# Two heads' products by turns: RWKV backs, block inversion and S5 output in a hybrid S5/RWKV-7 block

## The chip, the cores and the metric

The kernel runs on one core of a Trainium2 chip. The metric is the device time of one execution in microseconds (us). A core has a tensor engine for matrix products (PE; its weight loads are listed as PEld), a vector engine (DVE), a scalar engine (ACT), a general engine (POOL, GpSimd) and a queue engine (SP), each working through its own instructions in the order in which the program was written. PE writes its results to PSUM, which has eight banks; DVE and ACT read them from there.

## The reference, cut to what matters

One layer of a flow-matching block over 256 latent tokens and 256 context tokens, width 2048. A combined projection feeds an S5 branch (64 groups of 16 channels, 64 complex states each, both directions) and an RWKV-7 branch (16 heads of 64, both directions); gates, an output projection and a gated feed-forward part follow.

```
bu = jnp.einsum('lbgh,gph->lbgp', ugc, bbar)
states = s5_scan(bu, abar, s0[di])
y = y + jnp.real(jnp.einsum('lbgp,ghp->lbgh', states, cm))
...
def step(s, inp):
    r_t, w_t, k_t, v_t, kk_t, a_t = inp
    s_kk = jnp.einsum('bhvk,bhk->bhv', s, kk_t)
    s = s * w_t[:, :, None, :] - s_kk[..., None] * (kk_t * a_t)[:, :, None, :] + v_t[..., None] * k_t[:, :, None, :]
    return s, jnp.einsum('bhvk,bhk->bhv', s, r_t)
```

The kernel works out both recurrences over chunks: four tokens a chunk in S5, 64 tokens a chunk in RWKV, where the step inside a chunk becomes products with a 64 x 64 matrix and the inverse of a triangular one.

## The kernel before

**Dense stream.** All large projections run as one stream of weight tiles through PE. Each tile of 128 x 128 is split by ACT (`hi`) and DVE (`lo`) and used in three passes into accumulators `psacc`. In the order of time the stream holds the input projection (weights `win`), the modulation vector (weights `adaR`, used unsplit: a product of one column of `sc` with 256 columns of weights `w`, 768 instructions in the trace), the gated projection of S5 (`glu`), and the later projections. The input projection has 4 banks for `psacc` and 4 for everything else; the modulation part has 2 and 6.

**Background streams.** The S5 branch and the RWKV branch are Python generators that name the engine on which they go on, and how many free banks they need (`"tensor:1"`). `drive` writes them and the dense stream into one program; a rough clock of the engines in the code (class `Clock`) decides only what is written next. Once written, the order on each engine is fixed.

**S5 output** (`s5_out`). Eight slabs, one bank `psyp` each. A slab has four pairs of groups; the even group of a pair lies in partitions 0 to 63, the odd one in 64 to 127 (the parity, `par`). Each parity takes five products of 64 x 64 into its own half of the bank's partitions: one of `W` with `u`, and four of `wout` with the states `SB`.

**RWKV.** The work goes by pairs of heads, p = 0 to 7 for the context and 8 to 15 for the latent tokens, in both directions d; two pairs make a half (`h0` to `h7`). One head of a pair lies in partitions 0 to 63, the other in 64 to 127.

- `rw_front` makes the scaled vectors `H` and `KR` of a pair and direction, on ACT and DVE.
- `rw_back` makes the products inside the chunks: for each head four transposes (`ident`, in tile `cst`) and four products `H` x `KR`, of 64 rows by 128 columns. In the context one bank a head holds both (`pshg`); in the latent part, transposes (`pshp`) and products (`psgp`) have a bank each. ACT and DVE then take the results out. I call one call of it a back: 32 in all, 16 per segment.
- `rw_invert` inverts the triangular matrices of two halves, four times in all: a substitution of 31 steps on DVE (tiles `lth`, `Nh`), then products of 32 x 32 on PE, into `pswp` and, after a copy by ACT, into `pswq`; two banks (x = 0, 1) of each, with 16 products for either head in a bank.
- `rw_chain` carries the state over the four chunks of a half, with products `psxp`, `psup`, `pssp` and, in the latent part, `psy1` and `psy2`. Two halves run side by side.
- Halves 4 and 5 need the room of halves 0 and 1 (`rw_room`), so latent fronts begin after the first chains; pairs 4 to 7 of the context need room that comes free at the end of the input projection.

An fp32 product shows in the trace as two PE instructions with a weight load each; I call them passes. A transpose is one pass.

Of the kernel before, what the change touches and what calls it, by code (L numbers as in the profile page):

```python
# [17 lines left out]
P = 128  # L18
D = 2048
KT = 16  # L20
T = 256
C = 64
# [77 lines left out]
def lay_out(i):  # L100
    """Arrange the inputs for the program's loads: reshapes, transposes and copies only."""
# [78 lines left out]
class Clock:  # L180
    """A rough clock of the engines while the program is written: only the order of emission
    rests on it, never the result."""

    def __init__(self):
        self.t = dict(tensor=0.0, vector=0.0, scalar=0.0, gpsimd=0.0, sync=0.0)
        self.dma = self.hw = 0.0
        self.w = {}
        self.r = {}
        self.mark = 0.0
        self.table = None  # L190
        self.mms = 0
        self.tick, self.cols, self.full = 0, 0.0, False
        self.recent = deque()

    def array(self, t0, cost, cols):
        """Time of a product by the tensor engine's clock, which rests after a window of little use."""
        i = int(t0 / 3.4133)
        if i != self.tick:
            self.full = i == self.tick + 1 and self.cols >= 3060
            self.tick, self.cols = i, 0.0  # L200
        self.cols += cols
        cost = cost if self.full else 2 * cost
        self.recent.append((t0 + cost, cols))
        return cost

    def use(self, t):
        """Columns that have gone through the tensor engine in the window before t."""
# [13 lines left out]
    def cost(self, eng, op, out, a, k):  # L221
# [3 lines left out]
        if eng == "tensor":  # L225
# [7 lines left out]
            # the weights' way in counts as well  # L233
# [17 lines left out]
    def run(self, eng, op, a, k):  # L251
# [29 lines left out]
        if eng == "tensor":  # L281
            n = 1
# [67 lines left out]
class Dense:  # L350
    """Streams weights through the tensor engine: each weight tile is split exactly into two
    float32r parts and used in three passes; the activations come split the same way."""
# [24 lines left out]
    def open(self, first, cap, side=None):  # L377
        """Rings for the weights of the half-units from `first` up to `cap`, loaded and split ahead of
        their use."""
# [19 lines left out]
    def open_raw(self, pool, first, cap):  # L399
        """Loads in `pool` for the half-units that are used as they are."""  # L400
# [13 lines left out]
    def prep(self):  # L414
        """Split the next weight tile; a stream."""
# [19 lines left out]
    def evacuate(self):  # L435
        """Take the sums out, one after another; a stream."""
# [8 lines left out]
    def drop(self):  # L445
        """The sum has been read."""
        self.opened -= self.now
# [13 lines left out]
    def when(self):  # L461
        """When the weights of the next step will be there."""
# [5 lines left out]
    def step(self):  # L468
        """Emit a part of a half-unit: SUB weight tiles."""
# [39 lines left out]
class Bg:  # L509
    """A background stream: yields the engine that its next operations start on (with a + when others  # L510
    may go first), or a condition."""
# [22 lines left out]
class Flags(dict):  # L534
    """What has been emitted so far, with the time at which it will have come about."""
# [17 lines left out]
class Kernel:  # L553
# [24 lines left out]
    # y = 1/sqrt(v): exp(-ln/2), then one Newton step.  # L578
# [8 lines left out]
    def run(self):  # L587
        nc, tc, A = self.nc, self.tc, self.A
        es = ExitStack()
        with es:  # L590
# [31 lines left out]
            # scratch in DRAM  # L622
# [17 lines left out]
    # ------------------------------------------------------------------ dense jobs  # L640
    def make_jobs(self):
# [27 lines left out]
        # the first two features by turns: the last parts of the activations come late  # L669
# [22 lines left out]
    # ------------------------------------------------------------------ helpers  # L692
# [17 lines left out]
    def drive(self, until, must=(), all=True, span=None, stop=lambda: False, drain=True):  # L710
        """Interleave the dense stream, up to half-unit `until`, with the background streams; spread
        over `span`, if given, so that it lasts as long as they do."""
        d, c = self.dense, self.clk
        p0, t0 = d.pos, c.t["tensor"]
        while ((all and (d.pos < until or (drain and d.busy()))) or any(not b.done for b in must)) and not stop():
# [11 lines left out]
            # small products alone don't keep the tensor engine's clock up  # L727
# [3 lines left out]
            if dense and pick is not None and not pick.cond:  # L731
                # products that would wait for their weights hold up what comes after them
# [16 lines left out]
    def after(self, t):  # L749
        """Let the stream go on once what was written to `t` has landed."""  # L750
        self.clk.mark = max(self.clk.mark, self.clk.w.get(t.tensor.name, 0.0))

    def add_banks(self, es, n):
        """Banks that the background streams share."""
# [6 lines left out]
    def bank(self, shape, name):  # L761
        """The bank that has been free for longest."""
# [16 lines left out]
    def e_mod(self, b, acc):  # L779
        """Two features of the modulation that the later parts take, from a row to columns."""  # L780
# [16 lines left out]
    def mod_late(self, pool):  # L797
        """The rest of the modulation vector: a product along the weights' rows for every feature."""
# [33 lines left out]
    # ------------------------------------------------------------------ startup  # L832
    def startup(self, sp):
# [5 lines left out]
        # the parts of the modulation's weights, every fourth for the vector engine, and what comes  # L839
        # between them  # L840
# [46 lines left out]
        # 1 / rms of every token, the same on all partitions  # L887
# [46 lines left out]
        def scales(k0, n):  # L934
            # ada (raw products) + bias; A1 = norm1_w * (1 + scale)
# [77 lines left out]
    # ------------------------------------------------------------------ z evacuation  # L1013
# [11 lines left out]
    def mix(self, acc, mu, ctx=None):  # L1025
        """z + (neighbour mean - z) * mu for one 128-channel tile."""
# [70 lines left out]
    def z_gate(self, m, acc):  # L1097
        """The gates are kept as tanh(z / 2): sigmoid(z) = (tanh(z / 2) + 1) / 2."""
# [8 lines left out]
    # ------------------------------------------------------------------ S5  # L1107
    def small_exp(self, pool, x, out, tag):
        """exp on a small tile: range reduction and a polynomial, good to float32."""
# [33 lines left out]
    def s5_prep(self):  # L1143
# [17 lines left out]
        def out_matrices():  # L1161
            # output matrix: Re(C L^t s): rows re and -im
# [32 lines left out]
        # sine and cosine of a_im * dt through the half angle  # L1195
# [24 lines left out]
        # powers of abar (1..4), abar - 1 and the factor of the input matrix  # L1220
# [25 lines left out]
        # recurrence factors, laid as the states are: [re/im][gp][dir]  # L1246
# [5 lines left out]
        # power tables by slot: B: forward 3 - j, backward j; C: forward t + 1, backward 4 - t  # L1252
# [24 lines left out]
        def turned():  # L1277
            # transposed input matrix, the two groups of a pair in diagonal blocks, and the kernel's lags
# [40 lines left out]
            # y += d * u, as a part of the zero-lag block  # L1319
# [5 lines left out]
            # matrix inside a chunk: both directions' blocks, moved to the token that they belong to  # L1325
# [47 lines left out]
    def s5_in(self):  # L1373
        """What enters the states in every chunk, of both segments at once."""
# [54 lines left out]
    def s5_states(self):  # L1429
        """States after each chunk; the backward direction runs over the chunks from the end. Of the  # L1430
        context only the last state counts: chunks are joined in pairs, level by level."""
# [52 lines left out]
    def s5_out(self, pool, SB, u, W):  # L1484
# [13 lines left out]
        for sl in range(8):  # L1498
            yield "tensor:1", wos[2 * sl], wos[2 * sl + 1], u
            yp = self.bank([P, 4, 64], f"psyp{sl}")  # L1500
            for g in range(4):
                gp = 4 * sl + g
                wo = wos[gp // 2]
                for par in range(2):
                    ps = slice(64 * par, 64 * par + 64)
                    nc.tensor.matmul(yp[ps, g, :], lhsT=W[ps, gp, :], rhs=u[ps, gp, :], start=True, stop=False)
                    for d in range(2):
                        for ri in range(2):
# [12 lines left out]
    # ------------------------------------------------------------------ RWKV-7  # L1521
    # Halves of four heads go through the streams one after another: `front` and `back` prepare each
    # pair of heads, the chunk matrices of two halves are inverted together, the state is carried
    # over the chunks, and `post` finishes the output of the latent halves.
    def rw_norm(self, j):
        """Keys of a pair of heads in both segments, normalised per head."""
# [32 lines left out]
    def rw_load(self, st, a):  # L1559
        """Loads of one pair of heads."""  # L1560
# [25 lines left out]
    def rw_front(self, st, a, d):  # L1586
        """Everything of one pair of heads in one direction that doesn't need the state, up to the
        scaled vectors."""
# [67 lines left out]
    def rw_bonus(self, st, a):  # L1656
        """Sum over the head of r * (k_fwd + k_bwd) * r_k, times v."""
# [24 lines left out]
    def rw_tiles(self, st):  # L1682
        """What a half keeps for its state."""
# [16 lines left out]
    def rw_room(self):  # L1700
        """Room for the halves: all of the context's at first; latent ones as the context's end, the
        last in the place of the first."""
# [30 lines left out]
    def rw_vt(self, st, a):  # L1733
        """Values of one pair, transposed."""
# [25 lines left out]
    def rw_back(self, st, a, d):  # L1760
        """Products inside the chunks of one pair in one direction."""
# [10 lines left out]
        # every product into a bank comes before the first read of it, and each head has its banks:  # L1772
        # the two heads' rows go through the array side by side
        for h in range(2):
            oth = hs[1 - h]
            yield "tensor:1" if W == C else "tensor:2", H, KR[h]
            if W == C:
                bank = self.bank([P, 2, 4, C], f"pshg{n_}_{h}")
                hp, gps, held = bank[:, 0], bank[:, 1], [bank]
            else:  # L1780
                hp = self.bank([P, 4, C], f"pshp{n_}_{h}")
                gps = self.bank([P, 4, W], f"psgp{n_}_{h}")
                held = [hp, gps]
            for u in range(4):
                nc.tensor.transpose(hp[:, u, :], lhs(h, u), self.cs("ident")[hs[h], hs[h]])
            for u in range(4):
                nc.tensor.matmul(gps[:, u, :], lhsT=lhs(h, u), rhs=KR[h][hs[h], a, d, u, :], start=True, stop=True)
# [8 lines left out]
            # the substitution reads A^T below its diagonal only  # L1796
# [8 lines left out]
    def rw_invert(self, sts):  # L1805
        """T = (I + A)^-1 of every chunk of two halves: 32 x 32 blocks on the diagonal by substitution
        with a problem on each partition, the block below by two products; T^T replaces A^T."""
# [593 lines left out]
```

## Time and profile before

| | us |
|---|---|
| three runs | 2313.3, 2315.94, 2323.11 |
| median of the runs | 2315.94 |
| profiled execution, span of its trace | 2319.3 |
| PE busy | 2235.1 (96%) |
| DVE busy | 1484.2 (64%) |
| ACT busy | 1103.1 (48%) |

The profiled execution is described by its span, from its first instruction to its last; no other time belongs to it. It lies 3.4 us above the median of the runs and inside their extent. All rows further down are of this execution, and times in them count from its start. Three stretches matter: the S5 output at 645 to 712 us, the rest of the input projection to 803 us, and the RWKV recurrence beside the modulation product to 1277 us.

### The profile page before, as it was taken

To read this page: it belongs to the slowest core of one execution; us is meant where nothing else is said; L and a number is where in the kernel's file an instruction comes from. 1 tells how busy PE (TensorE), PEld (TensorE's weight loads), DVE (VectorE), ACT (ScalarE), POOL (GpSimd) and SP (SyncE) were. 2 spreads that over 40 slices of the span, in tenths; PEclk is the share of its full clock that TensorE was granted. 3 is DMA by queue.
4 is the path that set the end of the run, shared out by engine and by line. 5 is a ranking of instruction groups with operands and counts; after the bars stand their busy time and mean duration, and the time that the engine had idled before them with its cause. 6 is when DMAs were issued, how large, how long until landed. Compare 5 with 4: busy or idle time off the path is not lost.

```text
span 2319.3 us, 46718 instructions
## 1 busy us (share of the span) xinstructions
PE 2235.1 (96%) x19036; PEld 1966.2 (85%) x19036; DVE 1484.2 (64%) x2899; ACT 1103.1 (48%) x1908; POOL 150.9 (7%) x313
## 2 busy tenths in 40 slices
PE   7999999999999999999989799999999999999997
PEld 2289999999999865565736699999999999999997
DVE  3778848889835746677482557666666666554444
ACT  2335664334646657474635544454444444443333
POOL 0001210000101102010010100000000000000000
PEclk9999999999999979888898899999999999999999
DMA  9945565367764434535162675667777776556653
GB/s 372 341 145 189 197 203 181 110 193 213 231 196 131 131 115 120 163 97 173 56 196 87 184 256 183 183 207 227 228 229 227 229 226 182 182 182 183 183 183 133
DMA packets 155063, 431.92 MB, mean 186 GB/s; under 512 B 26272, under 2 KB 39584, under 8 KB 153952
## 3 DMA queue, kind: packets, MB, share of 16 engines
q1 hardware_dynamic: 130192, 360.76, 49.9%
q0 software_dynamic: 17600, 57.17, 7.6%
q10 hardware_dynamic: 7056, 11.01, 1.4%
q8 instruction: 149, 2.44, 0.4%
q14 instruction: 66, 0.54, 0.1%
HBM read 398.46 MB, written 30.41 MB: 185 GB/s over the span
## 4 chain that ended last, share of the span: by engine, by line
PE 77%; DVE 8%; issue 7%; ACT 4%; DMA 4%; POOL 0%; ACTq 0%; SPq 0%; DVEq 0%; POOLq 0%
PE psacc L312 63%; PE adacc L312 2%; PE psyp L312 2%; DVE lo L312 1%; PE pshg L312 1%; PE psbu L312 1%; DMA w<-in_win_dram 1%; PE pswph L312 1%; DMA ad<-in_adaP_dram 1%; PE psgp L312 1%; PE pswqh L312 1%; PE psss L312 1%; PE pslb L312 1%; DVE Nh L312 1%; PE psuph L312 1%
## 5 line engine op out<-in xcount | busy, mean ns | idle before, releaser
L312 DVE TENSOR_TENSOR lo<-w,hi 128x1024 fp32r<-128x1024 f32 x478 | 584.8, 1224 | 421.5 <-ACT hi L312 412.8
L312 ACT ACTIVATE hi<-w 128x1024 fp32r<-128x1024 f32 x478 | 504.8, 1058 | 679.5 <-PE psacc L312 566.2
L312 PE MATMUL psacc<-h,hi 128*128 128x258 f32 x2816 | 511.1, 284 | 1.2 <-ACT hi L312 1.2
L312 PEld LDWEIGHTS psacc<-h,hi 128*128 128x128 f32 x2816 | 438.4, 190 | 1.4 <-ACT hi L312 1.4
L312 PE MATMUL psacc<-hl,hi 128*128 128x256 f32 x2144 | 407.4, 284 | 0.0
L312 PE MATMUL psacc<-h,lo 128*128 128x258 f32 x1408 | 400.1, 284 | 0.8 <-DVE lo L312 0.8
L312 PEld LDWEIGHTS psacc<-hl,hi 128*128 128x128 f32 x2144 | 332.4, 191 | 6.3 <-issue 5.7
L312 PE MATMUL psacc<-hl,lo 128*128 128x256 f32 x1072 | 303.5, 283 | 0.4 <-DVE lo L312 0.4
L312 PEld LDWEIGHTS psacc<-h,lo 128*128 128x128 f32 x1408 | 267.6, 190 | 1.0 <-DVE lo L312 1.0
L312 PE MATMUL psacc<-hid,hi 128*128 128x256 f32 x1408 | 253.5, 283 | 0.0
L312 PEld LDWEIGHTS psacc<-hid,hi 128*128 128x128 f32 x1408 | 219.9, 192 | 0.0
L312 PE MATMUL psacc<-w,sc 128*1 128x256 f32 x768 | 201.3, 407 | 19.1 <-DVE ada L312 8.5
L312 PEld LDWEIGHTS psacc<-hl,lo 128*128 128x128 f32 x1072 | 204.7, 191 | 0.6 <-DVE lo L312 0.6
L312 PE MATMUL psacc<-hid,lo 128*128 128x256 f32 x704 | 199.5, 283 | 0.0
L312 PE MATMUL psacc<-hc,hi 128*128 128x256 f32 x832 | 173.0, 289 | 0.0
L312 PEld LDWEIGHTS psacc<-w,sc 128*1 128x1 f32 x768 | 57.8, 86 | 125.3 <-DMA w<-in_adaR_dram 22.7
L312 PEld LDWEIGHTS psacc<-hid,lo 128*128 128x128 f32 x704 | 135.4, 192 | 0.0
L312 PEld LDWEIGHTS psacc<-hc,hi 128*128 128x128 f32 x832 | 127.8, 189 | 2.3 <-issue 1.4
L312 PE MATMUL psacc<-hc,lo 128*128 128x256 f32 x416 | 116.2, 279 | 0.0
L312 PE MATMUL psacc<-gl,hi 128*128 128x256 f32 x512 | 99.0, 295 | 11.1 <-ACT hi L312 6.0
L312 PE MATMUL adacc<-ad,sc 128*2 128x512 f32 x192 | 88.3, 612 | 17.2 <-DMA ad<-in_adaP_dram 9.7
L312 PEld LDWEIGHTS psacc<-gl,hi 128*128 128x128 f32 x512 | 83.8, 200 | 13.2 <-ACT hi L312 6.2
(368 smaller groups left out, 3465.4 us busy)
## 6 DMA issues: line engine op xcount, KB each, us to landing
w<-in_w_dram SPq DMA_DIRECT2D x264, 512.0 KB, 4.3
w<-in_win_dram SPq DMA_DIRECT2D x134, 512.0 KB, 4.2
w<-in_adaR_dram SPq DMA_DIRECT2D x192, 256.0 KB, 2.9
ad<-in_adaP_dram SPq DMA_DIRECT2D x48, 512.0 KB, 6.8
w<-in_glu_dram SPq DMA_DIRECT2D x32, 512.0 KB, 4.0
w<-in_wo_dram SPq DMA_DIRECT2D x32, 512.0 KB, 3.6
adg<-in_adaG_dram POOLq DMA_DIRECT2D x32, 512.0 KB, 5.3
ad<-in_adaD_dram SPq DMA_DIRECT2D x16, 512.0 KB, 7.7
```

Of the source, the lines that this page charges most:

```text
L312: return f(*a, **k)
```

## The change

In the backs, the products of the two heads are written by turns, products ahead of transposes, and the stream asks for the banks of both heads at once: two in the context, four in the latent part. In the block inversion the loop over heads moves inside the loop over the 16 blocks, and in the S5 output the loop over parities inside that over the products. The code's rough clock counts the products of a back at 0.55 of their cost. The rest of the diff takes comments out.

```
+        self.side = 1.0
...
         c = self.cost(eng, op, out, a, k)
         if eng == "tensor":
+            c *= self.side
...
# s5_out
-                for par in range(2):
-                    ps = slice(64 * par, 64 * par + 64)
+                pss = [slice(64 * par, 64 * par + 64) for par in range(2)]
+                for ps in pss:
                     nc.tensor.matmul(yp[ps, g, :], lhsT=W[ps, gp, :], rhs=u[ps, gp, :], start=True, stop=False)
-                    for d in range(2):
-                        for ri in range(2):
+                for d in range(2):
+                    for ri in range(2):
+                        for ps in pss:
...
# rw_back
+        yield "tensor:2" if W == C else "tensor:4", H, KR[0], KR[1]
+        hps, gs, holds = [], [], []
         for h in range(2):
-            oth = hs[1 - h]
-            yield "tensor:1" if W == C else "tensor:2", H, KR[h]
             if W == C:
                 bank = self.bank([P, 2, 4, C], f"pshg{n_}_{h}")
...
-            for u in range(4):
-                nc.tensor.transpose(hp[:, u, :], lhs(h, u), self.cs("ident")[hs[h], hs[h]])
-            for u in range(4):
-                nc.tensor.matmul(gps[:, u, :], lhsT=lhs(h, u), rhs=KR[h][hs[h], a, d, u, :], start=True, stop=True)
...
+        self.clk.side = 0.55
+        for u in range(4):
+            for h in range(2):
+                nc.tensor.matmul(gs[h][:, u, :], lhsT=lhs(h, u), rhs=KR[h][hs[h], a, d, u, :], start=True, stop=True)
+        for u in range(4):
+            for h in range(2):
+                nc.tensor.transpose(hps[h][:, u, :], lhs(h, u), self.cs("ident")[hs[h], hs[h]])
+        self.clk.side = 1.0
+        for h in range(2):
+            hp, gps, held, oth = hps[h], gs[h], holds[h], hs[1 - h]
...
# rw_invert, pswp (and pswq in the same way)
-            for h in range(2):
-                r0 = slice(64 * h, 64 * h + 32)
-                r1 = slice(64 * h + 32, 64 * h + 64)
-                for u in range(16):
+            for u in range(16):
+                for h in range(2):
+                    r0 = slice(64 * h, 64 * h + 32)
+                    r1 = slice(64 * h + 32, 64 * h + 64)
                     nc.tensor.matmul(wp[r1, u, :], lhsT=AQ[x][r0, u, 32:64], rhs=t11[r0, :, 16 * x + u],
                                      start=True, stop=True, tile_position=(64 * h, 64 * h + 32))
```

The order of instructions is the same in both programs up to the first back, but for the turns in `psyp`. Here are PE's rows at that first back, in the input projection just after the S5 output; the numbers after `pshg` are pair, direction and head, and a last number counts tiles. Before:

```order
L312 MATMUL psss_8200<-nk_8032,cst 128x512
L312 MATMUL pshg_0_0_0_8210<-cst,H_0_0_8193 128x64 x4
L312 MATMUL pshg_0_0_0_8210<-KR0h_8184,H_0_0_8193 128x64 x4
L312 MATMUL pshg_0_1_0_8221<-cst,H_0_1_8196 128x64 x4
L312 MATMUL pshg_0_1_0_8221<-KR0h_8184,H_0_1_8196 128x64 x4
L312 MATMUL psvt_0_8231<-cst,v_0_6642 128x128 x2
...
L312 MATMUL pshg_0_0_1_8255<-cst,H_0_0_8193 128x64 x4
L312 MATMUL pshg_0_0_1_8255<-KR1h_8185,H_0_0_8193 128x64 x4
```

After, in the same place:

```order
L315 MATMUL psss_8200<-nk_8032,cst 128x512
L315 MATMUL pshg_0_0_0_8210<-KR0h_8184,H_0_0_8193 128x64
L315 MATMUL pshg_0_0_1_8211<-KR1h_8185,H_0_0_8193 128x64
...
L315 MATMUL pshg_0_0_0_8210<-cst,H_0_0_8193 128x64
L315 MATMUL pshg_0_0_1_8211<-cst,H_0_0_8193 128x64
...
L315 MATMUL psvt_0_8230<-cst,v_0_6642 128x128 x2
```

Before, the second head of pair 0 came twelve dense instructions and a transpose of values later; now it takes turns with the first, and the other direction's back has moved further down. From here on the order of the background streams differs throughout. The place that moves most is the end of the context's RWKV work: PE's rows around the last back of the context (`pshg0_7_1`) and the last step of the first two chains (`psxp…_3`, `pssp…_3`), with the numbers of half and step in the names. Before:

```order
L312 MATMUL psxph1_3_10315<-SV0h1_8337,KR0h1_8332 64x64
...
L312 MATMUL pshg0_7_0_1_10324<-KR1h3_9603,H00_7_0_10240 128x64 x4
L312 MATMUL psuph1_3_10335<-xsh1_3_10333,AQh1_8334 64x64 x8
...
L312 MATMUL pssph1_3_10370<-SV0h1_8337,HT0h1_8335 64x64
...
L312 MATMUL psmod2_10414<-cst_74,arow_79 128x1 x2
...
L312 MATMUL pshg0_7_1_0_10500<-KR0h3_9602,H10_7_1_10459 128x64 x4
L312 MATMUL pslb1_0_1_10514<-wad1_98,lw1_0_10162 128x256 x2
...
L312 MATMUL pshg0_7_1_1_10520<-KR1h3_9603,H10_7_1_10459 128x64 x4
```

After:

```order
L315 MATMUL psmod2_10255<-cst_74,arow_79 128x1 x2
...
L315 MATMUL pshg0_7_1_0_10358<-KR0h3_9460,H10_7_1_10314 128x64
L315 MATMUL pshg0_7_1_1_10359<-KR1h3_9461,H10_7_1_10314 128x64
...
L315 MATMUL pslb1_0_1_10383<-wad1_98,lw1_0_10144 128x256 x2
L315 MATMUL psxph0_3_10390<-SV0h0_8189,KR0h0_8184 64x64
...
L315 MATMUL psuph1_3_10439<-xsh1_3_10430,AQh1_8486 64x64 x8
...
L315 MATMUL pssph1_3_10471<-SV0h1_8489,HT0h1_8487 64x64
...
L315 MATMUL psmod3_10541<-cst_74,arow_79 128x1 x2
```

The context's last back stood behind the first chains' last step and now stands ahead of it, while the modulation product (`psmod` counts its features) has come equally far. In later inversions and chains the streams keep nearly the same places to each other.

## Rows read from the trace of the kernel before

**Rows 1.** Windows: length; busy us (PE, PEld, DVE, ACT, POOL); PEclk; DMA; GB/s

```profile
645.00:712.00 67.00, 66.77 (x815) 62.42 (x813) 19.79 (x28) 26.09 (x38) 5.35 (x10) 1.00 0.65 188
712.00:803.00 91.00, 89.22 (x707) 83.06 (x706) 66.90 (x131) 67.79 (x136) 14.14 (x33) 0.98 0.43 135
803.00:1277.00 474.00, 445.23 (x4642) 276.64 (x4642) 286.79 (x745) 257.71 (x591) 48.00 (x106) 0.88 0.41 125
```

**Rows 2.** Chain that ended last, two slabs of S5 output: start us, us, what

```profile
667.46 5.32 PE psyp L312 x66
672.78 2.34 PE psacc L312 x18
```

**Rows 3.** Timeline of PE, first slab of S5 output: start us, us, engine, instruction

```profile
648.55 0.33 PE L312 MATMUL psyp<-u,W 64*64 64x64 f32 x2
648.71 0.71 PE L312 MATMUL psyp<-SB,wout 64*64 64x64 f32 x5
649.15 0.27 PE L312 MATMUL psyp<-u,W 64*64 64x64 f32 x1
...
649.31 0.71 PE L312 MATMUL psyp<-SB,wout 64*64 64x64 f32 x7
649.75 0.27 PE L312 MATMUL psyp<-u,W 64*64 64x64 f32 x1
```

**Rows 4.** Timeline of PE, one head of a context back, and what follows

```profile
716.99 0.46 PE L312 MATMUL pshg<-cst,H 64*128 64x64 f32 x4 [0.31 <-ACT HT0h L312]
717.29 1.05 PE L312 MATMUL pshg<-KR1h,H 64*128 64x64 f32 x8
718.27 0.51 PE L312 MATMUL psacc<-hl,hi 128*128 128x256 f32 x2
```

**Rows 5.** Timeline of PE, two heads of a latent back that stand side by side

```profile
907.05 0.27 PE L312 MATMUL psgp<-KR0h,H 64*128 64x128 f32 x1
907.07 0.22 PE L312 MATMUL pshp<-cst,H 64*128 64x64 f32 x1
907.13 0.33 PE L312 MATMUL psgp<-KR1h,H 64*128 64x128 f32 x1
907.16 0.27 PE L312 MATMUL psgp<-KR0h,H 64*128 64x128 f32 x1
```

**Rows 6.** Timeline of PE, products of the first inversion

```profile
832.62 3.56 PE L312 MATMUL pswph<-t11h,AQh 32*32 32x32 f32 x64
...
844.05 2.11 PE L312 MATMUL pswqh<-AQh,w1h 32*32 32x32 f32 x64
...
849.17 3.43 PE L312 MATMUL pswqh<-AQh,w1h 32*32 32x32 f32 x64
```

**Rows 7.** Windows of tile pswp, then of pswq, in the recurrence

```profile
803.00:1277.00 474.00, 28.22 (x512) 27.23 (x512) 9.41 (x16) 0.88 0.41 125
...
803.00:1277.00 474.00, 25.74 (x512) 24.82 (x512) 9.39 (x16) 0.88 0.41 125
```

**Rows 8.** Timeline of PE, one step of a chain: both heads' products into one bank

```profile
870.98 0.68 PE L312 MATMUL psuph<-xsh,AQh 64*64 64x64 f32 x16
871.59 0.27 PE L312 MATMUL psxph<-SV0h,KR0h 128*64 128x64 f32 x1
871.60 0.27 PE L312 MATMUL psxph<-SV1h,KR1h 128*64 128x64 f32 x1
```

**Rows 9.** Windows of the recurrence: inversions' products, substitutions and chains by turns

```profile
857.70:900.00 42.30, 42.28 (x537) 30.89 (x536) 20.39 (x54) 31.40 (x85) 4.65 (x11) 0.88 0.24 69
900.00:963.90 63.90, 57.21 (x299) 26.25 (x300) 54.33 (x144) 30.12 (x69) 10.36 (x21) 0.95 0.63 192
963.90:990.00 26.10, 26.10 (x299) 19.88 (x298) 3.00 (x7) 12.24 (x22) 2.28 (x6) 0.56 0.22 67
...
1028.00:1087.30 59.30, 52.77 (x292) 25.95 (x290) 54.58 (x143) 28.55 (x64) 10.07 (x22) 1.00 0.64 189
...
1151.00:1224.50 73.50, 64.36 (x340) 29.13 (x338) 57.71 (x135) 33.90 (x61) 6.20 (x11) 1.00 0.58 182
```

More of the change, by code (lines that the diff above doesn't have):

```diff
@@ L1771, in rw_back @@
         lhs = lambda h, u: H[hs[h], u].rearrange("p s t -> p (s t)")[:, h * C:h * C + P]
+        yield "tensor:2" if W == C else "tensor:4", H, KR[0], KR[1]
+        hps, gs, holds = [], [], []
         for h in range(2):
-            oth = hs[1 - h]
-            yield "tensor:1" if W == C else "tensor:2", H, KR[h]
             if W == C:
                 bank = self.bank([P, 2, 4, C], f"pshg{n_}_{h}")
-                hp, gps, held = bank[:, 0], bank[:, 1], [bank]
-            else:
-                hp = self.bank([P, 4, C], f"pshp{n_}_{h}")
-                gps = self.bank([P, 4, W], f"psgp{n_}_{h}")
-                held = [hp, gps]
-            for u in range(4):
-                nc.tensor.transpose(hp[:, u, :], lhs(h, u), self.cs("ident")[hs[h], hs[h]])
-            for u in range(4):
-                nc.tensor.matmul(gps[:, u, :], lhsT=lhs(h, u), rhs=KR[h][hs[h], a, d, u, :], start=True, stop=True)
+                hps.append(bank[:, 0])
+                gs.append(bank[:, 1])
+                holds.append([bank])
+            else:
+                hps.append(self.bank([P, 4, C], f"pshp{n_}_{h}"))
+                gs.append(self.bank([P, 4, W], f"psgp{n_}_{h}"))
+                holds.append([hps[h], gs[h]])
+        self.clk.side = 0.55
[8 more added lines that the diff above has]
+            hp, gps, held, oth = hps[h], gs[h], holds[h], hs[1 - h]
             mask = self.cs("mask")
@@ L1871, in rw_invert @@
             wp = self.bank([P, 16, 32], f"pswq{n_}_{x}")
-            for h in range(2):
-                r0 = slice(64 * h, 64 * h + 32)
-                r1 = slice(64 * h + 32, 64 * h + 64)
-                for u in range(16):
+            for u in range(16):
+                for h in range(2):
+                    r0 = slice(64 * h, 64 * h + 32)
+                    r1 = slice(64 * h + 32, 64 * h + 64)
                     nc.tensor.matmul(wp[r0, u, :], lhsT=w1[r1, 16 * x + u, :], rhs=AQ[x][r1, u, 32:64], start=True, stop=True,
```

## Prediction

> **What bounds the kernel now.** I first read the windows of three stretches [rows 1]: how long each engine worked in the S5 output, the rest of the input projection and the RWKV recurrence. PE is busy 66.8 of 67 us, 89.2 of 91 and 445 of 474, so it pauses 29 us in the last stretch and hardly at all before. DVE works 287 of those 474 us, ACT 258. Then the chain of waits through the S5 output [rows 2]: a slab of `psyp` of 5.32 us, a piece of dense stream, the next slab, with no other engine between; what PE saves there is saved for good. The recurrence needs a finer cut, into the substitutions, the products of the inversions, and the chains [rows 9]. In the products' stretch at 964 us PE is busy throughout and DVE for 3 of 26 us. In a chain stretch PE is full and DVE works 20 of 42 us. In the substitutions DVE works 54.3 of 63.9, 54.6 of 59.3 and 57.7 of 73.5 us, while PE is filled with the modulation product: there DVE is about as close to the limit as PE.
>
> So PE's time counts fully in three kinds of stretch and badly in the fourth. The rest, the feed-forward part above all, isn't touched.
>
> **S5 output.** One parity alone shows at the head of the first slab [rows 3]: five passes over `SB` span 0.71 us with a last pass of about 0.27, so they follow at (0.71 - 0.27) / 4 = 0.11 us; the two `W` passes follow at 0.06. A parity's ten passes take 2 x 0.06 + 8 x 0.11 = 1.0 us. A new parity begins every 0.60 us (649.15, 649.75), since PE already starts the next parity in the other half of the array while the last passes of this one run; the seven passes in 0.71 us at 649.31 are of both. By turns, a pair of parities takes 1.0 instead of 1.2 us, and the tail at the slab's end goes: about 4.3 us a slab, 1.0 less, 8 in all. Bounds: 0 if the turns add nothing; 23 if a pass cost what it does in a chain, where 16 passes of both heads span 0.68 us, (0.68 - 0.27) / 15 = 0.027 [rows 8] (80 x 0.03 = 2.4 a slab). I take 8, because these passes already run at 0.11 in their own half and nothing shortens that.
>
> **Backs.** One head takes 1.28 us, from its first transpose at 716.99 to the next instruction at 718.27 [rows 4]: eight passes at (1.05 - 0.27) / 7 = 0.11 and four transposes at some 0.07. Do two heads that share all 128 columns but no rows go side by side? In one latent back they stood next to each other and PE ran them over the seam [rows 5]: passes of head 0 start at 907.05 and 907.16, 0.11 apart as if alone, while a transpose of head 1 and its first product start between them. So a back should take 1.28 us instead of 2.56. 32 backs x 1.28 = 41; the five that the order of before already shows with heads side by side had some 0.3 each, so 39.5. By the order 8 of the 32 stand in the input projection (10 us) and 24 in the recurrence (29.5). Lower bound 0, if seams are all that overlap.
>
> **Inversion.** `pswp` is busy for 28.2 us and `pswq` for 25.7 [rows 7], each in eight groups of 64 passes. A pass of `pswp` takes 0.05 us [rows 6]; `pswq` takes 2.11 us a group at the full clock and 3.43 when the clock has dropped. Each head has its own corner of the array, so by turns two passes go in the time of one: half of 53.9, 27 us. The nearest row for a bound is again the chain's 0.027 a pass: 64 x 0.027 = 1.7 a group, 28 for all, 26 saved; below, 0. I take 27.
>
> The Trainium skill's page "TensorEngine Tiling (Array Packing)", section "Restrictions and Gotchas", says that different row tiles cannot use one PSUM bank at the same time. That speaks against these two edits, in which both heads or parities write one bank, and not against the backs. The trace differs: in the chains the two heads' products go into one bank, from different rows of the array into different partitions, and 16 passes span 0.68 us [rows 8]. By the rule the sum would be 35 us smaller.
>
> **What is taken back.** Saved: 8 + 39.5 + 27 = 74.5 us. By the order of the changed program 15 of the 24 later backs stand inside a substitution, where DVE is near its limit [rows 9]; PE then waits instead: 15 x 1.28 = 19. The last back ahead of each of three substitutions still counts, and its evacuations with it, 4 us. So 15 us are lost, between 0 (PE has the modulation product to pull forward) and 19.
>
> **New waits.** A back now waits for both heads' `KR` and for two or four banks. Behind it on PE stand the next dense product and the chain's next step, and on that step wait ACT's copies and DVE's update of the state. I cost this at nothing, since the dense work written ahead of it covers it; were that cover gone, PE's idle time in the recurrence, 29 us [rows 1], might double: +29. The other way, the context's last back now comes ahead of the first chains' last step, so the second substitution, which began some 12 us behind them, can begin while DVE is half idle [rows 9]: up to 12 us gained. Both stay out of the sum and in the range. The products ahead of the transposes cost nothing: the same instructions in the same bank.
>
> **Sum.** 2319.3 - 74.5 + 15 = 2260 for the profiled execution. It lay 3.4 us above the median of the runs; the prediction for the median is **2256 us**, 2.6% faster.
>
> **Rivals**, in times of the median.
> - *More comes back.* The modulation product fills what the substitutions leave and the second one starts early: 74.5 + 12 = 87 us, 2229. For it: PE's work falls by that much whatever happens. Against: DVE's 85 to 92% in two substitutions.
> - *The recurrence's own chain decides.* Copies by ACT stand between `pswp` and `pswq`, and between the steps of a chain; with PE's work halved they lie bare. Left are 18 us before 803 and in the inversions 27 less some 3 for each of four copies: 33 us, 2283. For it: DVE and ACT are above half busy. Against: PE is full in chains and products [rows 9].
> - *One bank.* The rule above holds for these tiles: the 35 us fall away, 2291.
> - *The change doesn't do what it says*: whole streams don't overlap as the seam does, and the moves cancel: 2316. Against: rows 5 and 8 [rows 5, 8].
> - *Slower by the clock.* In the recurrence the granted clock averages 0.88 [rows 1], between the levels 1.2 and 2.4 GHz, and is lowest around the small products, 0.56 [rows 9]. Less work on PE could let it fall longer. At the full clock PE's 445 us are 392; 56 saved leave some 343. The stretch stays as long as now plus the 18 us won before it, with 29 idle, when the clock is 343 / 463 = 0.74; below that the kernel is slower, and at 0.70 it takes 490 + 29 - 18 = 501 us instead of 474, so 2343. Against: the low stretches are the small products, and these get shorter while the large ones stay.
>
> **Chances.** The forecast 0.56 (its own range 2242 to 2272), more 0.18, the chain 0.13, one bank 0.05, nothing 0.04, slower 0.04. With 0.5% (12 us) as what a measurement can tell from no change: faster 0.91, same 0.05, slower 0.04. The range that leaves out 2 in 10 runs from 2232, most of the "more" case, to 2290, which holds the chain's case.
>
> **What would show it.** Slabs of `psyp` of 4.3 us; backs with `KR0h` and `KR1h` passes by turns, 0.11 us apart within a head, 1.3 us for both heads; `pswp` groups of 1.8 us. The input projection should end some 18 us earlier, the last chain some 60. PE's busy time in the recurrence should fall towards 390 us with more idle time, DVE's stay near 287. I am wrong if passes of the two heads start 0.11 us apart from each other (no overlap), if the inversion's groups keep their 3.5 us while the backs halve (one bank), if PE's idle time in the recurrence grows by much more than 15 us (the chain), or if the granted clock falls under 0.8 (the clock).

## The result, and the profile after

| | before | changed |
|---|---|---|
| median of the runs, us | 2314.62 (2308.23 to 2323.11, 4 runs) | 2265.98 (2263.62 to 2268.66, 4 runs) |
| ratio, 95% interval | 1 | 0.978 (0.9761 to 0.9799) |
| profiled execution, span | 2319.3 | 2262.5 |
| PE busy | 2235.1 (96%) | 2151.0 (95%) |

The changed kernel is 2.2% faster; 2256 us was forecast. The medians lie 49 us apart, the spans of the two profiled executions 57: the first span lies 5 us above its runs' median, the second 3 us below. I read the changed kernel's trace in the order of the prediction. First the same three stretches [rows 1]; the columns are length, busy us of PE, PEld, DVE, ACT and POOL, granted clock, DMA share, GB/s:

```profile
645.70:703.70 58.00, 57.54 (x814) 53.10 (x813) 19.74 (x28) 26.26 (x38) 3.23 (x6) 1.00 0.73 211
703.70:786.30 82.60, 80.56 (x707) 74.74 (x706) 59.30 (x108) 67.17 (x134) 17.62 (x39) 0.98 0.49 155
786.30:1219.70 433.40, 379.06 (x4646) 220.50 (x4646) 293.89 (x769) 256.79 (x595) 46.77 (x104) 0.94 0.46 137
```

The input projection ends 17 us sooner (786 instead of 803 us), the last chain 57 us sooner (1219.7 instead of 1277). In the recurrence PE works 66 us less, but its idle time grows from 29 to 54 us. DVE works 7 us more. The rest, to the end of the program, takes as long as before (2262.5 - 1219.7 = 1043 us, and 2319.3 - 1277.0 = 1042).

The chain of waits through the S5 output has slabs of 4.15 us where it had 5.32 [rows 2]:

```profile
658.79 4.15 PE psyp L315 x80
662.94 3.06 PE psacc L315 x24
666.00 4.15 PE psyp L315 x80
```

On PE's timeline of the first back, the products of the two heads start at the same time, and those of one head follow at 0.11 us as before [rows 4]; a back takes some 1.3 us, where one head took 1.28:

```profile
704.26 0.27 PE L315 MATMUL pshg<-KR0h,H 64*128 64x64 f32 x1
704.27 0.27 PE L315 MATMUL pshg<-KR1h,H 64*128 64x64 f32 x1
704.37 0.27 PE L315 MATMUL pshg<-KR0h,H 64*128 64x64 f32 x1
704.38 0.27 PE L315 MATMUL pshg<-KR1h,H 64*128 64x64 f32 x1
...
704.71 0.41 PE L315 MATMUL pshg<-cst,H 64*128 64x64 f32 x8
```

In the inversion a group of `pswp` takes 1.98 us instead of 3.56 [rows 6], one of `pswq` 1.20 at the full clock and 1.92 at the lower one (granted clock 1.00 and 0.50 while they ran), instead of 2.11 and 3.43. First four rows of PE's timeline, then the windows of `pswp` and of `pswq` in the recurrence (28.2 and 25.7 us before [rows 7]):

```profile
824.35 1.98 PE L315 MATMUL pswph<-t11h,AQh 32*32 32x32 f32 x64
...
832.18 2.01 PE L315 MATMUL pswph<-t11h,AQh 32*32 32x32 f32 x64
...
840.35 1.92 PE L315 MATMUL pswqh<-AQh,w1h 32*32 32x32 f32 x64
...
1053.73 1.20 PE L315 MATMUL pswqh<-AQh,w1h 32*32 32x32 f32 x64
```

```profile
786.00:1219.60 433.60, 15.76 (x512) 0.94 0.46 137
786.00:1219.60 433.60, 12.38 (x512) 0.94 0.46 137
```

So all three overlaps are there, in the sizes forecast. The question that the profile leaves is what each of them is worth in the end, and where the 25 us of new idle time come from.

### The profile page after: what moved, and what is told of

Its sections match the earlier page's. It is cut to its first block, busy times and chain, and to the rows that moved or that the text cites. A ratio compares the mean times of both kernels' runs of the same rounds, so it can differ in the third digit from the quotient of the medians.

```text
span 2262.5 us, 46694 instructions
## 1 busy us (share of the span) xinstructions
PE 2151.0 (95%) x19036; PEld 1888.8 (83%) x19036; DVE 1484.1 (66%) x2899; ACT 1100.7 (49%) x1908; POOL 150.5 (7%) x312
## 4 chain that ended last, share of the span: by engine, by line
PE 74%; DVE 8%; issue 7%; ACT 6%; DMA 4%; POOL 0%; ACTq 0%; SPq 0%; DVEq 0%; POOLq 0%
PE psacc L315 63%; PE adacc L315 2%; ACT AQh L315 1%; PE psyp L315 1%; PE psbu L315 1%; DVE lo L315 1%; DVE Nh L315 1%; DMA nk<-d_kvr 1%; DMA ad<-in_adaP_dram 1%; PE psss L315 1%; DVE lth L315 1%; PE pshg L315 1%; PE pskps L315 1%; PE pslb L315 1%; DVE SC L315 1%
## 5 line engine op out<-in xcount | busy, mean ns | idle before, releaser
L315 PE MATMUL psacc<-w,sc 128*1 128x256 f32 x768 | 189.1, 388 | 14.4 <-DVE ada L315 5.5
L315 PE MATMUL adacc<-ad,sc 128*2 128x512 f32 x192 | 93.4, 643 | 13.3 <-ACT sc L315 7.3
```

The source lines that it names most:

```text
L315: return f(*a, **k)
```

## The experiments

Twelve kernels ran, in three groups, each group on one chip beside the kernel before. The ratios are to that group's own runs of before; the changed kernel's is 0.978. A gain in us over the kernel before is the ratio's share of its 2314 us; the plain difference of two medians can lie a few us off.

| what is by turns, in which order of work | median, us | before | ratio (95%) |
|---|---|---|---|
| S5 output; before's order | 2308.39 | 2313.6 | 0.9966 (0.9949 to 0.9983) |
| inversion; before's order | 2272.03 | 2313.6 | 0.9812 (0.9782 to 0.9841) |
| both; before's order | 2263.93 | 2315.02 | 0.9774 (0.9752 to 0.9795) |
| backs; changed order | 2289.63 | 2315.02 | 0.989 (0.9869 to 0.9911) |
| nothing; changed order | 2310.05 | 2313.6 | 0.9976 (0.996 to 0.9993) |
| S5 output and inversion; changed order | 2282.14 | 2313.6 | 0.9849 (0.9822 to 0.9875) |

**S5 output alone.** Only `s5_out` of the diff; every other instruction stands where it stood.

> The kernel before with the S5 output alone by turns; every engine's other instructions stand in the order of before. In the changed kernel a slab of psyp takes 4.22 us where it took 5.39, 9.3 us in all. If PE's time counts in full there, the time falls by 9 us, 0.4%. Rival: the first substitution, on DVE, starts hardly earlier and keeps the gain; then the input projection still ends 9 us sooner but the first inversion's products start only 4 us sooner, and the time falls by 4 us or less.

Measured: 0.34% less, 8 us (4 to 12 by the interval), and in the trace the first inversion's products begin 7 us sooner, at 825.5 instead of 832.6 us. That fits the gain counting in full better than the rival, which gave 4 us for both.

**Inversion alone.** Only `rw_invert` of the diff, in the order of before.

> The kernel before with the products of the inversion alone by turns; the order of all else is that of before. The 1024 passes took 53.9 us of PE. Theory that PE's time counts in full there: they fall to some 27 us and the time falls by 26 us, 1.1%. Rival, copies lie bare: PE now waits for ACT's copies between pswp and pswq, about 3 us at each of four inversions, and the time falls by some 14 us. Rival, one bank: both heads write one bank and the groups keep their 3.5 us; no change.

Measured: 1.9% less, 43 us (37 to 50 by the interval), more than PE's time in these products allows. The windows of the recurrence, all of it and then the modulation product's `psacc` alone:

```profile
801.20:1236.40 435.20, 405.08 (x4644) 244.48 (x4642) 287.32 (x745) 257.59 (x591) 48.31 (x106) 0.95 0.45 136
801.20:1236.40 435.20, 191.69 (x768) 0.95 0.45 136
```

The stretch is 39 us shorter than in before and PE works 40 us less, while its idle time stays at 30 us. By the windows of `pswp` and `pswq`, 15.70 and 11.09 us, the products give 27 of the 40. Another 10 come from the modulation product, which took 201.31 us in the 474 us of before for the same 768 instructions. The granted clock of the stretch is 0.95 instead of 0.88. So with this edit alone the clock is higher for what stands beside the products, which the prediction had priced at nothing.

**Each product of the inversion twice.** By turns, but with a second pass of every product into the same place:

```
-                for h in range(2):
+                for h, q in ((0, nc.tensor), (1, nc.tensor), (0, nc._nc.tensor), (1, nc._nc.tensor)):
...
-                    nc.tensor.matmul(wp[r1, u, :], ...
+                    q.matmul(wp[r1, u, :], ...
```

> The inversion alone by turns, as in the run that gave 2272 us, but every product is issued twice in turns (the second writes the same result again), so that these products take about as long on PE as before, with both corners of the array at work. Theory that the inversion alone saved 27 us of PE's time and some 15 us more by a higher granted clock, because both corners work at once: the 27 come back, the 15 stay, some 2299 us, with half-clock stretches as short as in the single run. Rival, all of it is time of the products and what waits for them: 2314 or more, with the granted clock of the recurrence back at 0.88.

Measured: 2311.04 us, 0.9979 (0.996 to 0.9997). In the profiled execution the products take 30.24 and 22.08 us, about as long as in before. The window of its recurrence:

```profile
799.20:1257.40 458.20, 429.31 (x5669) 265.79 (x5667) 286.95 (x745) 258.31 (x591) 48.03 (x106) 0.94 0.42 130
```

The median speaks for the rival: 39 of the 43 us are gone again. The profiled execution speaks for the theory: its span, 2299.0 us, lies 20 us above that of the inversion by turns, its clock in the recurrence stays at 0.94, and the modulation product takes 195.34 us. But it is the shortest of the 12 runs, which go from 2301 to 2319 us, and that of the inversion by turns is one of the two longest of its six (2263 to 2281 us). Over the whole program these two executions have the same mean granted clock, 0.980 and 0.979. The 12 runs lie between 0.968 and 0.980, the runs of before between 0.964 and 0.971, and those of the inversion by turns between 0.979 and 0.990. So the clock keeps its gain in some executions and loses most of it in others. Neither the duration of the products nor the two busy corners alone explain that, and what decides it stays open.

**S5 output and inversion, backs untouched, in the order of before.**

> The kernel before, its order kept, with the S5 output and the inversion by turns and the backs untouched. Alone these two gave 0.34% (8 us) and 1.9% (43 us). Theory: their gains add, since they stand in different stretches, and the time is 2314 - 51 = 2263 us, as good as the changed kernel (2266): then the backs by turns give nothing in all. Rival: the gains overlap as they do in the changed kernel's order, where both together gave 28 us: 2286, and the backs give the rest.

Measured: 2263.93 us, as good as the changed kernel. The gains add, and the backs by turns bring nothing on top.

**Backs alone.** `rw_back` and the price of 0.55 from the diff.

> The kernel before with the backs' change alone: both heads by turns, both claims at once, and the scheduler's lower price for them, hence the changed kernel's order of work. My prediction's term: 39.5 us of PE less 15 taken back, 2314 - 24 = 2290 us. By the run of the changed order without overlap (2310) and of the overlap in the changed kernel (16 us), 2294. Rival, PE's time counts in full: 2275. Rival, idle time takes all of it: 2310.

Measured: 1.1% less, 25 us, which is what the prediction's term gave (39.5 - 15). About 6 of them are the new order's, by the next run, so the overlap alone is worth some 20. Each part alone is worth its price or more, 8, 43 and 25 us, and all three together some 50 instead of 76.

**The changed order without any overlap**, and **with all but the backs' overlap.** The products of a back are put to the engine head by head, while the code's clock still counts them by turns, so that the rest keeps its place; in the first of the two, `s5_out` and `rw_invert` are those of before as well:

```
         for u in range(4):
             for h in range(2):
-                nc.tensor.matmul(gs[h][:, u, :], lhsT=lhs(h, u), ...
+                self.clk.run("tensor", "matmul", (gs[h][:, u, :],), ...
...
+        pe = nc._nc.tensor
+        for h in range(2):
+            for u in range(4):
+                pe.matmul(gs[h][:, u, :], lhsT=lhs(h, u), ...
+            for u in range(4):
+                pe.transpose(hps[h][:, u, :], lhs(h, u), ...
```

> The changed kernel's order of instructions on every engine and its claims of two and four banks at once, with nothing by turns: in the backs, the inversion and the S5 output one head or parity runs after the other. It shows what the order and the waits for banks are worth without any overlap. My prediction put both at nothing: 2316 us, within 6. Rival, earlier substitution: the order itself is worth up to 12 us, 2304. Rival, waits for banks: PE's idle time in the recurrence grows by up to 29 us, 2345.

> The changed kernel with its order and its banks, the S5 output and the inversion by turns, and only the backs' products head by head. Against the changed kernel (2266 us) it shows what the overlap of the backs alone is worth. If the prediction's term holds (39.5 us of PE less 15 taken back) it takes 2266 + 25 = 2291 us. Rival, PE's time counts in full: 2306. Rival, the substitutions on DVE decide and the backs are hidden beside them: 2275 or less.

Measured: 2310.05 and 2282.14 us. The order and the claims of several banks, taken together, cost nothing by themselves (0.24% gained, 6 us). In the changed order the backs' overlap is worth 16 us, and the S5 output and the inversion together 28, not the 51 that they gave in the order of before. The two orders, nearly equal with long products, part by 18 us once the S5 output and the inversion are by turns (2263.93 and 2282.14). So of the 26 us that the three gains lose together, most are lost between the new order and the other two edits, ahead of any overlap in the backs: 51 us become 28, while the backs' overlap falls only from 20 to 16.

**Does DVE's substitution take it back?** The changed kernel and its twin with the backs head by head, both without the operations of the substitution, which the code's clock still counts:

```
-            v.tensor_tensor(t3, L[:, j + 1:32, j:j + 1]...
-            v.tensor_tensor(N[:, j + 1:32, 0:m], N[:, j + 1:32, 0:m], t3, op=ALU.subtract)
```

> The changed kernel without the 62 operations of each substitution on DVE (84 us of DVE in all; the inverses are then those of the identity), every other instruction in the same order. It is to be read against the next run, its twin with the backs head by head. Theory: DVE in the substitutions takes back what the backs' overlap saves on PE, so without them the twins differ by the whole 32 us that the backs save (40 less what the seams gave), instead of 16. Rival: the order, the banks and the chain's copies take it back, and they differ by 16 us as before.

> The twin: order and banks of the changed kernel, S5 output and inversion by turns, the backs head by head, and no substitutions on DVE. Theory: slower than its twin by 32 us. Rival: by 16 us, as with the substitutions.

Measured: 2256.81 and 2272.58 us, against 2265.98 and 2282.14 with the substitutions. Each gains some 9 us for 74 us of DVE's work in the recurrence (its busy time there falls from 294 to 220 us), and the twins still differ by 16. The rival was right: DVE's substitution isn't what takes the gain of the backs' overlap back. Windows of the changed kernel from the first inversion's products to the second's, and on to the third's; then the same two of the twin, of the changed kernel without substitutions, and of the twin without them:

```profile
824.40:929.60 105.20, 94.05 (x1057) 53.25 (x1056) 67.65 (x181) 64.65 (x149) 16.31 (x36) 0.90 0.50 145
929.60:1043.80 114.20, 104.26 (x1145) 57.23 (x1144) 86.36 (x222) 70.38 (x171) 13.71 (x31) 0.99 0.54 160
```

```profile
833.10:941.70 108.60, 101.44 (x1055) 60.71 (x1054) 67.81 (x181) 65.26 (x150) 16.58 (x36) 0.89 0.47 141
941.70:1059.50 117.80, 113.08 (x1147) 65.02 (x1147) 87.21 (x224) 71.02 (x172) 14.38 (x33) 0.96 0.52 155
```

```profile
820.20:921.60 101.40, 93.39 (x1055) 52.43 (x1054) 48.85 (x116) 64.84 (x149) 16.32 (x36) 0.92 0.50 150
921.60:1035.40 113.80, 106.41 (x1147) 57.88 (x1148) 68.51 (x160) 70.24 (x170) 13.77 (x32) 0.96 0.54 161
```

```profile
834.00:938.70 104.70, 100.56 (x1055) 60.24 (x1054) 48.39 (x114) 65.17 (x150) 16.59 (x36) 0.90 0.49 145
938.70:1055.90 117.20, 112.97 (x1146) 65.02 (x1145) 69.57 (x162) 70.35 (x170) 14.68 (x33) 0.96 0.52 156
```

In the first of the two stretches the overlap saves 7.4 us of PE's work and 3.4 us of time. With DVE at 49 instead of 68 us of some 105, it saves 7.2 and 3.3: about half of PE's gain there turns into waits with either load on DVE. The view of PE's waits has them in small pieces. Here are the groups that differ, in the first of the two stretches (us in total, times, longest us), of the changed kernel, then of the twin:

```profile
PE pshg L315 <- ACT H L315: 3.2, 1, 3.2
PE psacc L315 <- DVE ada L315: 3.0, 3, 2.0
PE psuph L315 <- ACT xsh L315: 1.6, 4, 0.6
```

```profile
PE pshg L1801 <- ACT H L315: 2.2, 1, 2.2
PE psacc L315 <- DVE ada L315: 1.9, 3, 0.9
...
PE psuph L315 <- ACT xsh L315: 0.3, 1, 0.3
```

PE comes sooner to steps that wait for one copy of ACT or DVE each, and waits there.

**Is the cover used up?** In the changed kernel all 384 products of the modulation stand ahead of the last inversion; in the order of before with S5 output and inversion by turns, 16 stand behind its first products. Last stretch, from there to the end of the last chain: the changed kernel, that other one, then the changed order without any overlap:

```profile
1171.00:1219.60 48.60, 37.06 (x904) 32.31 (x904) 12.60 (x39) 29.20 (x65) 1.07 (x2) 0.84 0.14 42
```

```profile
1183.10:1225.80 42.70, 41.63 (x938) 31.59 (x937) 12.89 (x43) 25.20 (x61) 1.06 (x2) 0.96 0.25 81
```

```profile
1217.50:1268.70 51.20, 42.88 (x904) 38.35 (x904) 12.58 (x39) 29.04 (x65) 1.06 (x2) 0.81 0.13 39
```

PE stands idle for 11.5 of 48.6 us in the first and for 1.1 of 42.7 in the second. In the third no modulation product is left either, and PE is idle for 8.3 us: it is the new order that uses the cover up earlier, and not the shorter products. I gave the changed kernel a longer span for the modulation product:

```
-SPANS = (None,330,100)
+SPANS = (None,390,100)
```

> The changed kernel with the modulation product paced over a longer span (390 instead of 330 in the unit of the program's own clock), which leaves 12 of its 384 steps for the last inversion and chain, where the changed kernel has none and the order of before with S5 output and inversion by turns has 16. Theory: PE stands idle at the end because its cover is used up (about 20 us from 1155 to 1226 us); the 12 steps of 0.93 us go there and 8 to 11 us are saved, 2257 us. Rival: as much idle time opens in the earlier stretches, 2266.

Measured: 2257.06 us, 0.9754 (0.9731 to 0.9777). That is 9 us less than the changed kernel by the medians and 6 by the ratios, and the two intervals overlap. The last stretch in its windows, and PE's timeline of the last inversion, first of the changed kernel (in square brackets: idle before, and what ended it), then of this run:

```profile
1171.20:1216.90 45.70, 41.41 (x933) 31.97 (x932) 12.81 (x42) 26.65 (x63) 1.06 (x2) 0.96 0.21 65
```

```profile
1171.02 3.82 PE L315 MATMUL pswph<-t11h,AQh 32*32 32x32 f32 x128 [5.69 <-DVE t11h L315]
1177.71 0.31 PE L315 MATMUL pswqh<-AQh,w1h 32*32 32x32 f32 x2 [2.87 <-ACT w1h L315]
1178.32 3.62 PE L315 MATMUL pswqh<-AQh,w1h 32*32 32x32 f32 x126 [0.30 <-ACT w1h L315]
1183.64 0.48 PE L315 MATMUL psxph<-SV0h,KR0h 128*64 128x64 f32 x2 [1.70 <-ACT SV0h L315]
```

```profile
1171.22 3.80 PE L315 MATMUL pswph<-t11h,AQh 32*32 32x32 f32 x128
1174.95 3.35 PE L315 MATMUL psacc<-w,sc 128*1 128x256 f32 x8
1178.23 1.20 PE L315 MATMUL pswqh<-AQh,w1h 32*32 32x32 f32 x64
1179.36 1.02 PE L315 MATMUL psacc<-w,sc 128*1 128x256 f32 x4
1180.31 1.20 PE L315 MATMUL pswqh<-AQh,w1h 32*32 32x32 f32 x64
```

Where the copies `w1h` left PE idle there is work again, and the clock of the stretch goes from 0.84 to 0.96: `pswq` takes 2.4 us instead of 3.9. But the stretch as a whole is only 3 us shorter, 45.7 instead of 48.6, and the last inversion begins where it did. PE's idle time falls there from 11.5 to 4.3 us and grows by some 3 us in the stretches ahead, as the rival said in part. So the median came out as the theory had it, but the trace shows only 3 us of it at the place that the theory named.

**The inversion at the price of 0.55 as well**, and the same **with a longer span** (370 instead of 330):

```
             wp = self.bank([P, 16, 32], f"pswp{n_}_{x}")
+            self.clk.side = 0.55
...
+            self.clk.side = 1.0
```

> The changed kernel in which the program that sets the order also prices the inversion's products at 0.55, as it does the backs'. The instructions are the same, their order isn't. If the changed kernel's PE idle time in the recurrence (54 us of 433) comes from an order made with too long products, it gets shorter: 2255 us or less. Rival: the idle time is DVE's in the substitutions, and the order moves the time by a few us either way: 2266, within 8.

> The run that priced the inversion's products at 0.55 as well (2257 us), with the modulation product paced over 370 instead of 330, so that 16 steps instead of 6 lie behind the last inversion's first products. Theory of the missing cover: 6 to 9 us less, about 2250 us. Rival: no change, 2257, within 6.

Measured: 2256.85 us, 0.975 (0.973 to 0.977), and 2272.93 us, 0.9817 (0.9791 to 0.9843). The first lies 9 us under the changed kernel by the medians, as the one with more cover does, but not by its last stretch:

```profile
1165.20:1215.40 50.20, 40.34 (x921) 32.48 (x920) 13.09 (x42) 28.02 (x64) 1.06 (x2) 0.93 0.15 48
```

That stretch is no shorter and PE is idle in it for 9.9 us; the last inversion begins 6 us sooner than in the changed kernel, at 1165.2 instead of 1171.0 us. The second was a miss. Its last stretch is as short and as full as the theory wanted, but in the profiled execution the clock fell in the four stretches ahead of it, to between 0.87 and 0.91. Its six runs go from 2266 us at a mean clock of 0.976 to 2280 us at 0.970, and the profiled one, 2277 us, is among those at 0.970. Its windows from the first inversion's products to the second's, and the last stretch:

```profile
821.80:932.00 110.20, 93.67 (x1037) 53.47 (x1038) 68.94 (x184) 68.31 (x153) 15.16 (x34) 0.87 0.44 130
...
1188.40:1229.80 41.40, 40.00 (x938) 31.08 (x936) 12.87 (x43) 27.27 (x64) 0.32 (x1) 1.00 0.25 79
```

So more cover for the last inversion isn't a gain in itself: it is taken from elsewhere, and the stretches there can get longer at a lower clock. Of the two gains of 9 us the cover explains some 3 in the one and none in the other; the rest may be a luckier spread of the products, which these runs don't settle.

## Why the prediction was right, and where its steps were not

- **What bounds the kernel:** right for the S5 output and the inversion, where what PE saves is saved (8 and 43 us alone). For the input projection only in part. It ended 17 us sooner, but the changed kernel's first inversion begins no sooner than that of the kernel without turns in the backs (824.4 and 824.1 us). PE does more of the modulation product in between, 92 passes instead of 69, and that is what it lacks at the end. The changed order without any overlap has the same 92.
- **S5 output, 8 us:** right. Slabs of 4.15 us in the chain, 9 us of PE's time, 8 us alone (4 to 12).
- **Backs, 39.5 us of PE's time:** right in size. `pshg` fell from 20.73 to 11.47 us in the input projection and from 23.39 to 15.03 in the recurrence, by the windows of that tile; `psgp` fell from 38.27 to 20.69 and `pshp` from 15.46 to 7.72: 43 us in all. Two heads do go side by side when they share all columns and no rows.
- **Inversion, 27 us:** right for PE's time in the products (53.9 to 28.1), mis-sized as a term: alone it took off 43 us. What lay beside it ran at a higher clock, 10 us in the modulation product alone, and I had put the clock down only as a risk. Why the clock rose is open.
- **The one-bank rule** (Trainium skill, "TensorEngine Tiling (Array Packing)", "Restrictions and Gotchas"), that different row tiles can't use one bank at the same time: the trace doesn't agree. Both heads' row tiles write one bank, into different partitions, and a group of `pswp` went from 3.56 to 1.98 us.
- **Taken back, 15 us:** this is the step that failed. I put it on DVE's substitutions; without them the overlap of the backs is worth the same 16 us. The idle time grew by 25 us and not by some 15, which is also what I had named as a sign of the chain's rival. About 10 us of it stand in the last stretch, where the modulation product had run out, some 7 of them already in the order without overlap. The rest is spread over the four stretches ahead (2, 4, 3 and 6 us). In the two whose waits were compared with the twin's, PE waits longer for single copies of ACT and DVE in the first, and for the transfers of the modulation weights in the other (3.2 instead of 1.1 us). Which wait decides, the runs don't show.
- **New bank waits and the order, nothing:** right as long as nothing overlaps (2310.05 against 2313.6). With the S5 output and the inversion by turns the order costs 18 us, about what the backs' overlap then brings back.
- **The sum:** 2260 forecast for the profiled execution, 2262.5 measured. The terms of PE's time held; two errors cancelled, the clock's 12 us in the modulation product (201 to 189) in favour and 10 us more idle time against. For the median another step failed: I took 3.4 us off because the profiled execution of before lay above its median, but that of the changed kernel lies 3.5 below. So the median fell by 49 us, 10 or so less than forecast. 2265.98 lies inside the range, and that the span came out so near is partly luck.

That the backs bring nothing beyond the other two parts, in the order that comes with them, I had not foreseen. Each part was priced against the kernel before, with the order of before still in place. The S5 output and the inversion give 51 us in that order and 28 in the new one.

## What to carry to other kernels

Price the parts of a change one after the other, not each against the kernel before: three gains of 8, 43 and 25 us gave some 50 together. Run the new order of work by itself too, and then with each part: by itself it cost nothing here, and with the inversion short it cost 18 us. Where a long product serves as filler, look at the place at which it runs out; a new order can move that place forward, and the last serial stretch lies bare; filling it again shortened that stretch by 3 us here. Look also at what stands beside small products at a low granted clock: shortening those products by 27 us here took another 10 us off the modulation product.

## What the runs showed of the hardware

- A group of 64 passes of `pswp` took 1.98 us at a granted clock of 1.00 and 2.01 at 0.50, `pswq` 1.20 and 1.92: of two products of the same size only one follows the clock. One difference between them is how the moving operand lies: `t11` is read with a stride, `AQ` isn't. No run tests whether that is the reason.
- With 27 us less of the inversion's products, the time fell by 43 us (37 to 50) and the granted clock of the recurrence rose from 0.88 to 0.95. With the products lengthened again by 25.5 us, 39 of these 43 us came back by the median, but only 20 between the two profiled executions, whose mean clocks over the program are the same (0.979 and 0.980).
- Two heads' products whose weights share all 128 columns but no rows ran side by side in separate banks: both heads' 24 passes took 1.3 us, where one head's 12 took 1.28. Products from different rows into different partitions of one bank did so too (`pswp` 1.98 instead of 3.56 us).
- A longer pacing of the filler came with 9 us less by the medians in one order and 16 more in a slightly different one. In the profiled execution of the loss the granted clock of the four stretches ahead of the last inversion lay between 0.87 and 0.91, where it had been between 0.90 and 0.99.
